# First feed-forward stage begun with six weight blocks per k-tile in six PSUM banks instead of four, with another warm-up operand and another order of the first loads

## Chip, core and metric

The kernel runs on one core of one Trainium2 chip. The metric is device time in microseconds (us); lower is better. Three timed runs of the kernel before gave 985.97, 986.46 and 987.25 us, median 986.46. PE is the matrix engine, DVE the vector engine, ACT the scalar engine, POOL the general engine, SP the engine that only issues transfers here.

## What is computed

A two-layer streaming-encoder trunk on 256 tokens of width 1024, all in float32. The stage that matters here is the first of four feed-forward blocks:

```python
def rms_norm(x, g):
    xf = x.astype(jnp.float32)
    y = xf * lax.rsqrt(jnp.mean(xf * xf, axis=-1, keepdims=True) + NORM_EPS)
    return (y * g.astype(jnp.float32)).astype(x.dtype)

def swiglu(x, w_in, w_out):
    gate, up = jnp.split(x @ w_in, 2, axis=-1)
    return (jax.nn.silu(gate) * up) @ w_out
...
    h = x
    for i in range(DEPTH):
        h = h + 0.5 * swiglu(rms_norm(h, ffn_norm[i, 0]), ffn_w_in[i, 0], ffn_w_out[i, 0])
...
    return rms_norm(h, final_norm)
```

`w_in` is 1024 x 5632 (2816 gate and 2816 up columns), `w_out` 2816 x 1024.

## The kernel before

Activations lie transposed: channels on the 128 partitions in 8 k-tiles (`KD`), the 256 tokens (`T`) along the free axis. Float32 products are made from pairs: a weight block `raw` is rounded to float32r as `whi` on ACT (line 97, or line 1099 for the first blocks), and the remainder `wlo = raw - whi` is taken on DVE (line 101, or line 228). The normalised input has the same two parts in `u` (high part on ACT, line 287; low part on DVE, line 292). For each k-tile and each block of 128 output columns PE runs a pair of matmuls: `whi` times both parts of `u` (512 columns, line 247) and `wlo` times the high part (256 columns, line 248). Here this is called **a pair**; a whole block is 8 pairs.

A feed-forward block has 22 (`KF`) gate blocks and 22 up blocks. Block c makes one PSUM bank `pg` and one bank `pu` (8 pairs each). Seven banks are in rotation, plus one small bank. The 1/rms of a token is not applied to the input but afterwards: DVE multiplies a finished bank by `rb`, the 1/rms of each token laid across all partitions (line 388, result `two`), which frees the bank.

Weights come through the class `Weights`. `plan` lists all weight blocks in order of use. `fetch` issues their transfers on SP (line 88) into four `raw` buffers; `begin` makes `whi` and `pump` makes `wlo` and then calls `fetch`; seven `whi`/`wlo` buffers exist. A block can be begun only if a buffer of the seven is free, that is, if `begun` is below the oldest block still in use (or the next to be got) plus 7.

The first stage is written out by hand (lines 1074 to 1133). `lead` holds, for each k-tile, the input's 256 columns and 4 blocks of weights (gate and up of c = 0 and c = 1): 768 columns, 384 KB, for k = 1 to 7 in one transfer each (line 1078); k = 0 comes in two pieces (lines 188 and 189). Behind them SP issues two weight blocks (line 1080), the two halves of `xt` (line 1082; the same input with tokens on the partitions, called `tokens`), then two more weight blocks. Meanwhile PE runs 16 warm-up matmuls on `warm`, a tile of zeros that DVE writes (lines 1086 to 1090). `first` (line 1106) then works k-tile by k-tile into four banks: for k = 0 the products one kind after the other (line 1110), for each later k four pairs. After k = 1 it squares `tokens` on ACT with a running sum (line 1124, two instructions); after k = 4, `by_token` puts on DVE `v = sums / 1024 + eps` (line 321) and on POOL `rtok = v ** -0.5` (line 326). At k = 1, 3, 5 and 7 `W.pump()` runs. Next come gate and up of c = 2, and then `by_column` (line 331): PE multiplies `rtok`, spread along the free axis, with the identity into the bank `pb`, and ACT copies `pb` to `rb` (line 334). After that the banks of c = 0, 1, 2 are multiplied by `rb` one after the other.

Each engine's instructions stand in one fixed order; the order follows the program text, except that the recording layer may place engines' instructions against each other by readiness.

Of the kernel before, what the change touches and what calls it, by code (L numbers as in the profile page):

```python
# [13 lines left out]
BF16 = mybir.dt.bfloat16  # L14
# [5 lines left out]
P = 128  # L20
D = 1024
T = 256
# [15 lines left out]
G_Q = 72  # L38
G_KV = 74
GAINS = 80  # L40

FV = (H + D) // 3

# [97 lines left out]
def trunk(ctx, tc, xT, xt, pT, pos, freq, bf, lead0, lead1, ffn_in, ffn_out, w_down, w_uq, w_ukv, mla_o,  # L141
# [13 lines left out]

    def plan_ffn(i):

        plan.extend(ffn_in[0, c] for c in range(0 if i else KD // 2))
        plan.extend(ffn_in[i, c] for c in range(0 if i else 4, 2 * KF))
        for d in range(KD):  # L160
            plan.extend(ffn_out[i, d, :, a * P:min(a + KD, KF) * P] for a in range(0, KF, KD))

# [18 lines left out]
    plan.extend(ple_rows[c, k] for c in range(2) for k in range(KD // 2))  # L181


    ROW = T + 4 * P
    lead = big.tile([P, 2 * KD + KD * ROW + 2 * D], F32, name="lead", tag="big")

    a, b = 2 * KD + T + 2 * P, 2 * KD + ROW
# [193 lines left out]
    def ffn(norm, nxt, then=None, first=None, meanwhile=None, later=None, soon=True):  # L381
        hs = big.tile([P, KF, 2, T], F32R, name="hs", tag="big")
        meanwhile = meanwhile or iter(())
        gu, hid = {}, {}

        def evacuate(c, i, ps):
            two = work.tile([P, 2, T], F32, name="two", tag="pair2", bufs=4)
            nc.vector.tensor_mul(two, ps, norm.rb2)  # L388
            gu[c, i] = tmp("gu")
            nc.gpsimd.tensor_add(gu[c, i], two[:, 0, :], two[:, 1, :])  # L390

        def hidden(c):
            h = hid.pop(c)
            split(hs[:, c, 0, :], hs[:, c, 1, :], h)

        def gate(c, ps, pumps=1):
            evacuate(c, 0, ps)
            W.pump(pumps)
            if c:
                hidden(c - 1)  # L400
            sg = tmp("sg")
            nc.scalar.activation(sg, gu.pop((c, 0)), AF.Silu)
            gu[c, 0] = sg

        def up(c, ps, pumps=1):
            evacuate(c, 1, ps)
            hid[c] = tmp("hid")
            nc.gpsimd.tensor_mul(hid[c], gu.pop((c, 0)), gu.pop((c, 1)))  # L408
            W.pump(pumps)
            if c % 2:  # L410
                W.catch_up()
            if first and c == 8:

                nc.sync.dma_start(state, xT)

        waits = [(bank("pg"), bank("pu"))]
        if first:
            waits.append((bank("pg"), bank("pu")))
            first([p for ps in waits for p in ps])
        else:  # L420
            blocks(waits[0], norm.pair)
            W.pump()
            if soon:
                norm.everywhere()
            W.pump()
        at = len(waits)
        for c in range(at, KF):
            pg = bank("pg")
            block(pg, norm.pair)
            if c == at:  # L430
                if soon and not first:
                    norm.turned_back()
                    gate(0, waits[0][0])
                    up(0, waits[0][1])
                    waits.clear()
                else:
                    if not first:
                        norm.everywhere()
                    W.pump()
            else:  # L440
                gate(c, pg)
            pu = bank("pu")
            block(pu, norm.pair)
            if c == at:
                if first:
                    norm.by_column()
                elif not soon:
                    norm.turned_back()
                for x, ps in enumerate(waits):
                    gate(x, ps[0], x)  # L450
                    up(x, ps[1], 0)
                gate(c, pg)
            up(c, pu, 0 if waits and c == at else 1)
        for d in range(KD):
            ps = bank("po")
            for a in range(0, KF, KD):
                w, = W.get()
                part(ps, w, hs, range(a, min(a + KD, KF)), KF - 1, at=lambda k: (k - a) * P)
                W.done(w)
                if a + KD < KF:  # L460
                    W.pump()
                    if d == a == 0:
                        hidden(KF - 1)
                    for _ in range(2):
                        next(meanwhile, None)
            for i in range(2):
                nc.vector.scalar_tensor_tensor(hT[:, d, :], ps[:, i, :], 0.5, hT[:, d, :], op0=ALU.mult, op1=ALU.add)  # L467
            if d < KD - 1:
                nxt.high(d, hT[:, d, :])
                W.pump()  # L470
                nxt.low(d, hT[:, d, :])
                nxt.square(hT[:, d, :])
            else:
                nxt.last(d, hT[:, d, :])
                W.pump()
            W.catch_up()
            if d == 1 and then:
                table(then)
            for _ in range(2):
                next(meanwhile, None)  # L480
            if later:
                later(d)
        for _ in meanwhile:
            pass
# [588 lines left out]

    tokens = lead[:, 2 * KD + KD * ROW:].rearrange("p (t d) -> p t d", t=2)
    steps = lead[:, 2 * KD:2 * KD + KD * ROW].rearrange("p (k n) -> p k n", k=KD)
    W.skip(KD // 2)
    for k in range(1, KD):
        nc.sync.dma_start(steps[:, k, :], lead1[k - 1])
    for t in range(2):
        nc.sync.dma_start(*W.raw())  # L1080
    for t in range(2):
        nc.sync.dma_start(tokens[:, t, :], xt[t])
    W.fetch()
    n0 = Norm(G_FFN, KD, D, table=lead)

    warm = const.tile([P, T], BF16, name="warm")
    nc.vector.memset(warm, 0.0)
    cold = bank("cold", (P, T))
    for _ in range(16):
        nc.tensor.matmul(cold, warm[:, :P], warm, start=True, stop=True)  # L1090
    for k in range(KD):
        if k % 2 == 0:
            hi, lo = W.pair()
        c = slice(k % 2 * 4 * P, (k % 2 + 1) * 4 * P)
        n0.high(k, steps[:, k, :T], vector=k == 0)

        n = 4 * P if k else 2 * P
        for a in range(0, 4 * P, n):
            nc.scalar.activation(hi[:, c][:, a:a + n], steps[:, k, T + a:T + a + n], AF.Copy)  # L1099
        n0.low(k, steps[:, k, :T])  # L1100
        rest(hi[:, c], lo[:, c], steps[:, k, T:])
        if k % 2:
            W.loaded += 1

    def first(ps):
        w, = W.get()

        for x, y, z in ((1, 0, 0), (1, 1, 1), (2, 0, 1)):
            for i, p in enumerate(ps):
                nc.tensor.matmul(p[:, z, :], w[x][:, i * P:(i + 1) * P], n0.pair[:, 0, y, :], start=z == 0,  # L1110
                                 stop=False)
        for k in range(1, KD):
            if k % 2 == 0:
                w, = W.get()
            for i, p in enumerate(ps):
                part(p, w, n0.pair, range(k, k + 1), KD - 1, at=lambda x: (k % 2 * 4 + i) * P)
            if k % 2:
                W.done(w)
                W.pump()
            if k == 1:  # L1120

# [124 lines left out]
def _layout(x, p, positions, ffn_norm, ffn_w_in, ffn_w_out, mix_norm, mla_w_down, mla_q_norm, mla_w_uq,  # L1246
# [15 lines left out]

    w = ffn_w_in.reshape(4, KD, P, 2, KF, P)

    lead = w[0, :, :, :, :2].transpose(0, 1, 3, 2, 4).reshape(KD, P, 4 * P)
    lead = np.concatenate([xT.reshape(P, KD, T).transpose(1, 0, 2), lead], axis=2)
    a["lead0"] = np.ascontiguousarray(np.concatenate([g[:, :2 * KD], lead[0]], axis=1))
    a["lead1"] = np.ascontiguousarray(lead[1:])
# [53 lines left out]
```

## Time and profile before

| | |
|---|---|
| median of three timed runs | 986.46 us |
| profiled execution, own time | 986.36 us |
| span of the profiled execution | 984.5 us |
| time outside the span | 1.86 us |
| 16 warm-up matmuls begin on PE | 1.08 us into the span |
| first weight matmul begins | 4.33 us |
| `pb` begins on PE | 22.96 us |
| granted TensorE clock, mean | 0.999 |

The profile gives, for one execution, the busy time of each engine, a list of who waited for whom, and a timeline. In a timeline row the columns are: start in us from the start of the span, duration in us, engine, line, operation, written tile <- read tiles, shapes, count; in brackets at the end the idle time of the engine before it and what ended that. A name such as `SPq` is the engine's issuing side. KB means 1024 bytes in the sizes of transfers; rates in GB/s are in 10^9 bytes.

### The profile page before, as it was taken

How to read it: one execution, taken by the hardware profiler on the slowest of the kernel's cores; microseconds unless marked ns; L12 is line 12 of the kernel's file. 1: busy time of each engine (PE TensorE's matmuls, PEld its weight loads, DVE VectorE, ACT ScalarE, POOL GpSimd, SP SyncE). 2: the span in 40 equal slices, each digit the busy share in tenths (PEclk: the TensorE clock that was granted, in tenths of full speed). 3: DMA queues.
4: the chain of work that ended last, by engine and by line, in shares of the span. 5: the costliest groups of instructions: out<-in, count | busy, mean ns of one | idle time of the engine just before them, and what ended most of it. 6: DMA issues, size and time to landing. Idle time of an engine off the chain costs nothing.

```text
span 984.5 us, 15920 instructions
## 1 busy us (share of the span) xinstructions
PE 975.1 (99%) x5762; PEld 861.6 (88%) x5762; DVE 741.8 (75%) x1099; ACT 510.2 (52%) x798; POOL 438.1 (44%) x370
## 2 busy tenths in 40 slices
PE   9999999999999999999999999999999999999997
PEld 7888888998988888889888888889889888888886
DVE  6777878686887887666877886666897878876585
ACT  7555544466565454545555454546445555445361
POOL 0777731110377765111477773122231677772120
PEclk9999999999999999999999999999999999999999
DMA  8576666573376665665366666556773666666571
GB/s 317 184 252 209 204 181 188 182 208 117 125 218 213 194 187 177 190 205 172 107 195 211 196 185 196 178 174 224 235 224 112 214 210 204 193 176 198 142 256 54
DMA packets 67006, 187.26 MB, mean 190 GB/s; under 512 B 18628, under 2 KB 21072, under 8 KB 66800
## 3 DMA queue, kind: packets, MB, share of 16 engines
q1 hardware_dynamic: 65904, 183.94, 60.3%
q0 software_dynamic: 448, 1.45, 0.5%
q8 instruction: 46, 0.75, 0.3%
q10 hardware_dynamic: 576, 0.85, 0.3%
q14 instruction: 32, 0.26, 0.1%
HBM read 181.62 MB, written 2.24 MB: 187 GB/s over the span
## 4 chain that ended last, share of the span: by engine, by line
PE 94%; DVE 2%; ACT 1%; issue 1%; DMA 1%; POOL 0%; SPq 0%; POOLq 0%; DVEq 0%; ACTq 0%
PE po L247 17%; PE pu L247 16%; PE pg L247 16%; PE po L248 8%; PE pg L248 8%; PE pu L248 8%; PE ps L247 5%; PE ps L248 2%; PE ps L234 2%; PE ps L232 2%; PE ps L233 2%; PE pv L232 1%; PE pv L234 1%; PE po L557 1%; PE pv L233 1%
## 5 line engine op out<-in xcount | busy, mean ns | idle before, releaser
L101 DVE TENSOR_TENSOR wlo<-raw,whi 128x1024 fp32r<-128x1024 f32 (+2 forms) x339 | 415.0, 1230 | 27.9 <-ACT whi L97 27.1
L97 ACT ACTIVATE whi<-raw 128x1024 fp32r<-128x1024 f32 (+2 forms) x339 | 339.5, 1025 | 91.7 <-PE pg L247 35.5
L390 POOL TENSOR_TENSOR gu<-two 128x256 f32<-128x256 f32 x176 | 233.4, 1327 | 115.4 <-DVE two L388 107.8
L247 PE MATMUL pg<-u,whi 128*128 128x512 f32 x702 | 251.4, 395 | 0.3 <-DVE u L292 0.2
L247 PE MATMUL pu<-u,whi 128*128 128x512 f32 x702 | 250.9, 395 | 0.0
L247 PE MATMUL po<-hs,whi 128*128 128x512 f32 x704 | 246.8, 394 | 0.0
L248 PE MATMUL pg<-u,wlo 128*128 128x256 f32 x702 | 197.1, 281 | 0.6 <-DVE wlo L101 0.5
L248 PE MATMUL po<-hs,wlo 128*128 128x256 f32 x704 | 197.2, 280 | 0.0
L248 PE MATMUL pu<-u,wlo 128*128 128x256 f32 x702 | 196.8, 280 | 0.0
L247 PEld LDWEIGHTS po<-hs,whi 128*128 128x128 f32 x704 | 132.1, 188 | 31.3
L247 PEld LDWEIGHTS pg<-u,whi 128*128 128x128 f32 x702 | 131.8, 188 | 31.7 <-ACT whi L1099 0.5
L247 PEld LDWEIGHTS pu<-u,whi 128*128 128x128 f32 x702 | 131.8, 188 | 31.0
L248 PEld LDWEIGHTS pg<-u,wlo 128*128 128x128 f32 x702 | 132.0, 188 | 1.6 <-DVE wlo L101 0.8
L248 PEld LDWEIGHTS po<-hs,wlo 128*128 128x128 f32 x704 | 132.3, 188 | 0.0
L248 PEld LDWEIGHTS pu<-u,wlo 128*128 128x128 f32 x702 | 132.0, 188 | 0.0
L303 POOL TENSOR_TENSOR acc<-acc,sq 128x256 f32<-128x256 f32 x42 | 45.7, 1089 | 174.5 <-ACT sq L298 153.0
L408 POOL TENSOR_TENSOR hid<-sg,gu 128x256 f32<-128x256 f32 x88 | 112.7, 1281 | 6.9
L228 DVE TENSOR_TENSOR hs<-hid,hs 128x256 fp32r<-128x256 f32 x88 | 59.7, 679 | 57.3 <-ACT hs L224 57.3
L224 ACT ACTIVATE hs<-hid 128x256 fp32r<-128x256 f32 x88 | 36.5, 414 | 115.1 <-POOL hid L408 114.8
L388 DVE TENSOR_TENSOR two<-pg,rb 128x512 f32<-128x512 f32 x88 | 60.3, 685 | 32.1 <-PE pg L248 31.7
L287 ACT ACTIVATE u<-state 128x256 fp32r<-128x256 f32 x47 | 24.0, 511 | 102.9 <-DVE state L467 82.6
L467 DVE SCALAR_TENSOR_TENSOR state<-po,state 128x256 f32<-128x256 f32 x64 | 27.2, 424 | 57.3 <-PE po L248 56.1
(258 smaller groups left out, 1160.1 us busy)
## 6 DMA issues: line engine op xcount, KB each, us to landing
raw<-in_ffn_in_dram SPq DMA_DIRECT2D x172, 512.0 KB, 4.2
raw<-in_ffn_out_dram SPq DMA_DIRECT2D x64, 512.0 KB, 3.7
raw<-in_ffn_out_dram SPq DMA_DIRECT2D x32, 384.0 KB, 3.5
raw<-in_fox_qk_dram SPq DMA_DIRECT2D x16, 512.0 KB, 4.7
raw<-in_mla_o_dram SPq DMA_DIRECT2D x8, 512.0 KB, 4.4
raw<-in_ple_gate_dram SPq DMA_DIRECT2D x8, 512.0 KB, 4.3
raw<-in_fox_o_dram SPq DMA_DIRECT2D x8, 512.0 KB, 4.3
raw<-in_ple_rows_dram SPq DMA_DIRECT2D x8, 512.0 KB, 4.3
```

The costliest lines, as they stand in the source:

```text
L97: self.nc.scalar.activation(self.pairs[i][0][:, c], self.raws[i][:, c], AF.Copy)
L101: self.nc.vector.tensor_sub(lo[:, c], self.raws[i][:, c], hi[:, c].bitcast(F32))
L224: nc.scalar.activation(hi, src, AF.Copy)
L228: nc.vector.tensor_sub(lo, src, hi.bitcast(F32))
L232: nc.tensor.matmul(ps, w[0], x[0], start=first, stop=False)
L233: nc.tensor.matmul(ps, w[1], x[0], start=False, stop=False)
L247: nc.tensor.matmul(ps, hi, x[:, k], start=k == 0, stop=False)
L248: nc.tensor.matmul(ps[:, 1, :], lo, x[:, k, 0, :], start=False, stop=k == last)
L303: nc.gpsimd.tensor_add(new, self.acc, sq)
L388: nc.vector.tensor_mul(two, ps, norm.rb2)
L390: nc.gpsimd.tensor_add(gu[c, i], two[:, 0, :], two[:, 1, :])
L408: nc.gpsimd.tensor_mul(hid[c], gu.pop((c, 0)), gu.pop((c, 1)))
```

## The change

`LEAD = 3` replaces the fixed two: `lead` now holds 6 blocks of weights per k-tile (gate and up of c = 0, 1, 2), 1024 columns or 512 KB for each of k = 1 to 7; the second piece of k = 0, on ACT's queue, grows from 256 to 512 columns. Each k-tile has a `whi`/`wlo` buffer of its own (before, two k-tiles shared one), so the plan skips 8 entries, not 4, and every k-tile counts as one loaded block. `first` works into six banks. `by_column` stands directly behind `first`. The two weight blocks that were issued ahead of `xt` are issued behind it. The warm-up reads the constant 1 that the preamble writes on POOL, and the memset of `warm` goes.

```diff
-        plan.extend(ffn_in[0, c] for c in range(0 if i else KD // 2))
-        plan.extend(ffn_in[i, c] for c in range(0 if i else 4, 2 * KF))
+        plan.extend(ffn_in[0, c] for c in range(0 if i else KD))
+        plan.extend(ffn_in[i, c] for c in range(0 if i else 2 * LEAD, 2 * KF))
...
-    ROW = T + 4 * P
+    ROW = T + 2 * LEAD * P
...
         if first:
-            waits.append((bank("pg"), bank("pu")))
+            waits.extend((bank("pg"), bank("pu")) for _ in range(1, LEAD))
             first([p for ps in waits for p in ps])
+            norm.by_column()
...
             if c == at:
-                if first:
-                    norm.by_column()
-                elif not soon:
+                if not (first or soon):
                     norm.turned_back()
...
-    W.skip(KD // 2)
+    W.skip(KD)
     for k in range(1, KD):
         nc.sync.dma_start(steps[:, k, :], lead1[k - 1])
-    for t in range(2):
-        nc.sync.dma_start(*W.raw())
     for t in range(2):
         nc.sync.dma_start(tokens[:, t, :], xt[t])
     W.fetch()
...
-    warm = const.tile([P, T], BF16, name="warm")
-    nc.vector.memset(warm, 0.0)
+    warm = nc.const_aps.tensor(1.0, [P, T], BF16)
...
-        if k % 2 == 0:
-            hi, lo = W.pair()
-        c = slice(k % 2 * 4 * P, (k % 2 + 1) * 4 * P)
+        hi, lo = (x[:, :2 * LEAD * P] for x in W.pair())
...
-        n = 4 * P if k else 2 * P
-        for a in range(0, 4 * P, n):
-            nc.scalar.activation(hi[:, c][:, a:a + n], steps[:, k, T + a:T + a + n], AF.Copy)
+        for a, b in ((0, 2 * LEAD),) if k else ((0, 2), (2, 2 * LEAD)):
+            nc.scalar.activation(hi[:, a * P:b * P], steps[:, k, T + a * P:T + b * P], AF.Copy)
...
-        rest(hi[:, c], lo[:, c], steps[:, k, T:])
-        if k % 2:
-            W.loaded += 1
+        rest(hi, lo, steps[:, k, T:])
+        W.loaded += 1
...
+        W.done(w)
         for k in range(1, KD):
-            if k % 2 == 0:
-                w, = W.get()
+            w, = W.get()
             for i, p in enumerate(ps):
-                part(p, w, n0.pair, range(k, k + 1), KD - 1, at=lambda x: (k % 2 * 4 + i) * P)
+                part(p, w, n0.pair, range(k, k + 1), KD - 1, at=lambda x: i * P)
+            W.done(w)
             if k % 2:
-                W.done(w)
                 W.pump()
...
-    lead = w[0, :, :, :, :2].transpose(0, 1, 3, 2, 4).reshape(KD, P, 4 * P)
+    lead = w[0, :, :, :, :LEAD].transpose(0, 1, 3, 2, 4).reshape(KD, P, 2 * LEAD * P)
```

The next rows are what SP issues first, from the start of the program, of the kernel before (rows of equal instructions are joined with their count):

```order
L188 DMA lead<-in_lead_dram 128x528
L1078 DMA lead<-in_lead_dram 128x768 x7
L1080 DMA raw<-in_ffn_in_dram 128x1024 x2
L1082 DMA lead<-in_xt_dram 128x1024 x2
L88 DMA raw<-in_ffn_in_dram 128x1024 x21
L414 DMA state<-in_xT_dram 128x2128
```

And the same place of the changed kernel:

```order
L190 DMA lead<-in_lead_dram 128x528
L1079 DMA lead<-in_lead_dram 128x1024 x7
L1081 DMA lead<-in_xt_dram 128x1024 x2
L90 DMA raw<-in_ffn_in_dram 128x1024 x23
L416 DMA state<-in_xT_dram 128x2128
L90 DMA raw<-in_ffn_in_dram 128x1024 x15
```

The two transfers of `xt` moved ahead of all weight blocks, and the seven of `lead` grew by a third.

On ACT, behind the last rounding of `lead`, before (`raw_105` and `raw_107` are the first two weight blocks, `raw_111`, `raw_113` and `raw_214` the next; the row with `sums` is the two squares of `tokens`; `rb` is the copy of `pb`):

```order
L97 ACTIVATE whi_207<-raw_105 128x1024
L97 ACTIVATE whi_210<-raw_107 128x1024
L1124 ACTIVATE lead_80,sums_216<-lead_80 128x1024 x2
L97 ACTIVATE whi_235<-raw_111 128x1024
L97 ACTIVATE whi_261<-raw_113 128x1024
L97 ACTIVATE whi_283<-raw_214 128x1024
L97 ACTIVATE whi_306<-raw_239 128x1024
L334 ACTIVATE rb_332<-pb_329 128x256
```

The same place in the changed kernel, where the weight blocks are, in order, `raw_107`, `raw_109`, `raw_111`, `raw_113` and `raw_229`:

```order
L99 ACTIVATE whi_225<-raw_107 128x1024
L1118 ACTIVATE lead_80,sums_231<-lead_80 128x1024 x2
L99 ACTIVATE whi_258<-raw_109 128x1024
L99 ACTIVATE whi_261<-raw_111 128x1024
L99 ACTIVATE whi_295<-raw_113 128x1024
L99 ACTIVATE whi_325<-raw_229 128x1024
L336 ACTIVATE rb_334<-pb_331 128x256
```

The rounding of the second weight block stood ahead of the squares and now stands behind them; the first one still stands ahead of them.

On DVE, at the place where `v` is made from the sums, before:

```order
L101 TENSOR_TENSOR wlo_208<-raw_105,whi_207 128x1024
L101 TENSOR_TENSOR wlo_211<-raw_107,whi_210 128x1024
L321 TENSOR_SCALAR v_249<-sums_216 128x2
L101 TENSOR_TENSOR wlo_236<-raw_111,whi_235 128x1024
L101 TENSOR_TENSOR wlo_262<-raw_113,whi_261 128x1024
L101 TENSOR_TENSOR wlo_284<-raw_214,whi_283 128x1024
L388 TENSOR_TENSOR two_334<-pg_183,rb_332 128x512
```

And in the changed kernel:

```order
L103 TENSOR_TENSOR wlo_226<-raw_107,whi_225 128x1024
L103 TENSOR_TENSOR wlo_259<-raw_109,whi_258 128x1024
L323 TENSOR_SCALAR v_279<-sums_231 128x2
L103 TENSOR_TENSOR wlo_262<-raw_111,whi_261 128x1024
L103 TENSOR_TENSOR wlo_296<-raw_113,whi_295 128x1024
L103 TENSOR_TENSOR wlo_326<-raw_229,whi_325 128x1024
L390 TENSOR_TENSOR two_376<-pg_189,rb_334 128x512
```

The order of kinds is the same: `v` stands behind the remainders of two weight blocks in both. What changed is on ACT: the second of those remainders now reads a rounding that stands behind the squares.

More of the change, by code (lines that the diff above doesn't have):

```diff
@@ L40 @@
 GAINS = 80
+LEAD = 3
 FV = (H + D) // 3
```

## Prediction

> **What bounds the kernel now.** I read the page's head and its chain of waits first, then PE's list of waits, then the timeline of the first 27 us engine by engine.
>
> ```profile
> span 984.5 us, 15920 instructions
> PE 975.1 (99%) x5762; PEld 861.6 (88%) x5762; DVE 741.8 (75%) x1099; ACT 510.2 (52%) x798; POOL 438.1 (44%) x370
> PE 94%; DVE 2%; ACT 1%; issue 1%; DMA 1%; POOL 0%; SPq 0%; POOLq 0%; DVEq 0%; ACTq 0%
> ```
>
> PE is busy 99% of the span and 94% of the chain that ended last, so a change pays only where it moves PE, and what PE loses early is not made up later. PE's own waits over the whole span are few:
>
> ```profile
> PE cold L1090 <- DVE warm L1087: 1.1, 1, 1.1
> PE pg L248 <- DVE wlo L101: 0.5, 1, 0.5
> PE pg L247 <- DVE u L292: 0.2, 1, 0.2
> PE pg L248 <- DVE wlo L228: 0.2, 1, 0.2
> PE po L557 <- ACT ptS L545: 0.2, 1, 0.2
> ```
>
> Here the columns are total us, number of waits, longest. The change touches the first, third and fourth, all of them in the first 10 us. So the gain has a ceiling near 2 us, and the question is what new wait can stand against it. A tile's 1/rms is the candidate: `pb` on PE waits for `rtok` on POOL, and everything on PE stands behind `pb`. These rows are POOL, DVE and PE at that place:
>
> ```profile
> 18.52 0.71 POOL L326 TENSOR_TENSOR rtok<-v,mhalf 128x2 f32<-128x2 f32 x1 [16.88 <-DVE v L321]
> 18.19 0.17 DVE L321 TENSOR_SCALAR v<-sums 128x2 f32<-128x2 f32 x1 [1.34 <-ACT lead L1124]
> 22.96 0.61 PE L331 MATMUL pb<-ident,rtok 128*128 128x128 f32 x4
> 23.32 0.48 PE L247 MATMUL pg<-u,whi 128*128 128x512 f32 x1
> 26.21 0.40 PE L247 MATMUL pu<-u,whi 128*128 128x512 f32 x1
> ```
>
> `rtok` was ready at 18.52 + 0.71 = 19.23, and PE asked for it at 22.96: the chain has 3.73 us to spare before.
>
> **How late PE asks after the change.** Ahead of `pb` stands the same amount of work: before, 4 blocks x 8 k-tiles + 16 pairs of c = 2 = 48 pairs; after, 6 x 8 = 48. (For k = 0, three matmuls of 256 columns stand for a pair.) What differs is when the early tiles arrive.
>
> ```profile
> 4.97 0.51 ACT L287 ACTIVATE u<-lead 128x256 fp32r<-128x256 f32 x1 [0.53 <-DMA lead<-in_lead_dram]
> 5.39 0.61 ACT L1099 ACTIVATE whi<-lead 128x512 fp32r<-128x512 f32 x1
> 7.27 0.51 ACT L287 ACTIVATE u<-lead 128x256 fp32r<-128x256 f32 x1 [1.27 <-DMA lead<-in_lead_dram]
> ...
> 8.34 0.69 DVE L228 TENSOR_TENSOR wlo<-lead,whi 128x512 fp32r<-128x512 f32 x1
> ...
> 9.08 0.39 PE L248 MATMUL pg<-u,wlo 128*128 128x256 f32 x1 [0.17 <-DVE wlo L228]
> ...
> 9.30 0.39 PE L247 MATMUL pu<-u,whi 128*128 128x512 f32 x1
> ```
>
> From 9.30 PE runs 39 pairs (3 left of k = 2, 20, 16) until 22.96: 0.350 us a pair. The waits for transfers are at 4.97 (k = 1, behind 264 + 128 + 384 = 776 KB) and 7.27 (k = 2, behind 1,160 KB). After, k = 1 ends behind 264 + 256 + 512 = 1,032 KB; between those two points that is about 4.97 + 2.30 x 256/384 = 6.5. Then 0.42 to the rounding, 0.83 for 768 columns (0.61 for 512, 1.06 for 1024 in the row below), 0.97 for `wlo` of 768 (0.69 for 512, 1.25 for 1024): `wlo` at 8.8, the second pair at 9.0, and 41 pairs more: PE asks for `pb` at 9.0 + 14.35 = **23.4**. The bounds are k = 1 at 5.6 and at 7.27: 22.5 to 24.1. So the six banks alone are worth between 0.5 gained and 1.2 lost, best value 0.4 lost: the wait at k = 2 goes, one at k = 1 of the same kind comes.
>
> **When `rtok` is ready after the change.** This decides. The rows of ACT and DVE on the path, before:
>
> ```profile
> 13.26 1.06 ACT L97 ACTIVATE whi<-raw 128x1024 fp32r<-128x1024 f32 x1 [0.22 <-DMA raw<-in_ffn_in_dram]
> 14.53 1.06 ACT L97 ACTIVATE whi<-raw 128x1024 fp32r<-128x1024 f32 x1 [0.21 <-DMA raw<-in_ffn_in_dram]
> 15.76 1.06 ACT L1124 ACTIVATE lead<-lead 128x1024 f32<-128x1024 f32 x1 [0.17 <-DMA lead<-in_xt_dram]
> 16.73 0.19 ACT L1124 ACTIVATION_READ_ACCUMULATOR lead<-lead 128x1 f32 x1
> 17.01 1.06 ACT L1124 ACTIVATE lead<-lead 128x1024 f32<-128x1024 f32 x1
> 17.98 0.18 ACT L1124 ACTIVATION_READ_ACCUMULATOR lead<-lead 128x1 f32 x1
> 19.83 1.06 ACT L97 ACTIVATE whi<-raw 128x1024 fp32r<-128x1024 f32 x1 [1.67 <-DMA raw<-in_ffn_in_dram]
> 21.18 1.06 ACT L97 ACTIVATE whi<-raw 128x1024 fp32r<-128x1024 f32 x1 [0.29 <-DMA raw<-in_ffn_in_dram]
> ...
> 14.35 2.50 DVE L101 TENSOR_TENSOR wlo<-raw,whi 128x1024 fp32r<-128x1024 f32 x2 [0.33 <-ACT whi L97]
> ```
>
> The transfers are one behind the other, and ACT waits for each. `xt` is fetched sooner in order but not in bytes: before, 392 + 7 x 384 + 2 x 512 + 2 x 512 = 5,128 KB end with it; after, 520 + 7 x 512 + 2 x 512 = 5,128 KB. It lands when it did, by 17.0. But on ACT the first weight block's rounding stands ahead of the squares in both, and that block now lands *behind* `xt`, as the 5,640th KB: before, that place was the third block's, and ACT got it at 19.83. So I take 19.83 for it. From there, by the rows:
>
> - rounding of block one at 19.83; the next ACT instruction 0.97 later (16.73 - 15.76, the same size): first square 20.80
> - two squares 15.76 to 18.16, so 2.40: done 23.20
> - rounding of block two starts there (its data, as the fourth block's before, came by 21.18)
> - its remainder on DVE 1.09 later (13.26 to 14.35): 24.29, taking 1.25: 25.54
> - `v` behind it in DVE's order, although its sums are ready since 23.20: 25.54
> - POOL starts 0.33 after `v` starts (18.19 to 18.52) and takes 0.71: **`rtok` at 26.58**, against 19.23 before.
>
> PE, asking at 23.4, stands for 3.2 us. `pb` at 26.62 instead of 22.96: **+3.66 us**.
>
> **What is late behind it.** The fourth up block (`pu` of c = 3) reuses the bank of the first gate block, so it waits for the first `two`, as before:
>
> ```profile
> 20.92 3.82 DVE L101 TENSOR_TENSOR wlo<-raw,whi 128x1024 fp32r<-128x1024 f32 x3 [2.56 <-ACT whi L97]
> 25.05 0.69 DVE L388 TENSOR_TENSOR two<-pg,rb 128x512 f32<-128x512 f32 x1 [0.31 <-ACT rb L334]
> 24.65 0.37 ACT L334 ACTIVATE rb<-pb 128x256 f32<-128x256 f32 x1
> ```
>
> Before, `two` ended at 25.74 and PE needed the bank at 26.21. After, `v` ends at 25.71, three remainders (3.82) stand ahead of `two` until 29.53, `two` ends 30.22; PE gets there at 26.62 + (26.21 - 22.96) = 29.87. So **+0.35** more. ACT's copy `rb` is not later than DVE: three roundings of 0.97 from 24.17 end at 27.1, `rb` is done by 27.5. Behind that the banks are freed faster than PE fills them, as before. Weight blocks only gain time while PE stands.
>
> **The remaining edits.** The memset of `warm` held PE until 1.08; DVE's first instruction of the program is at 0.80, so warm-up can begin up to 0.28 earlier. With the early matmuls at half pace for as long, that is worth at most 0.15 us, and the 128 KB more on ACT's queue can cost the first matmul about 0.3 (131,072 bytes at about 400 GB/s). Both lie ahead of the wait at `pb`, which swallows either sign, so I put them at 0; without that cover they are -0.15 and +0.3. Later order on DVE and ACT differs where two-block counts became one-block counts; PE's only later waits are 0.5 and 0.2, so I allow 0.5 either way and take 0.
>
> **Sum.** Against the profiled execution's own 986.36 (span 984.5 + 1.86; the median of the timed runs is 986.46, the same for this purpose): 3.66 + 0.35 = +4.0, so **990.3 us**, +0.40%.
>
> **Rivals.** *The late block lands earlier.* The third block's landing at 19.83 is 2.8 us behind `xt`, where its neighbours took 1.25. In that stretch one transfer of the instruction queue q8 appears, and the mean rate stays high:
>
> ```profile
> DMA packets 337, 1.25 MB, mean 416 GB/s; under 512 B 35, under 2 KB 35, under 8 KB 336
> ...
> q8 instruction: 1, 0.02, 2.1%
> ```
>
> 512 KB at 416 GB/s is 1.26 us. If that hindrance falls on another transfer, block one lands at 17.0 + 1.25 = 18.25 and everything moves with it: `rtok` 25.0, +2.1 at `pb`, +0.3 behind: 988.8. For it: the instructions' transfer follows PE's progress, which is a little different now. Against it: by my count PE is at nearly the same instruction then.
>
> *No stall, so not slower.* `rtok` comes before PE asks if block one lands before 23.4 - 6.8 = 16.6. Then only the early terms count: +0.4 (-0.5 to +1.2), 986.8. Larger packets could carry the lead faster than the early dip before, but 5,640 KB at 416 GB/s (13.9 us) behind a first landing wait of 3.7 us leaves little room. That the change works as its parts suggest, with the early waits gone and the clock up 0.3 us sooner, lies at the lower end of this case: 985.9 or less.
>
> *The clock drops in the stall.* Before, the matmuls after warm-up keep a slow pace until 5.5, that is 4.5 us after PE began:
>
> ```profile
> 5.33 0.41 PE L1110 MATMUL pg<-u,whi 128*128 128x256 f32 x1
> 5.54 0.37 PE L1110 MATMUL pu<-u,whi 128*128 128x256 f32 x1
> 5.75 0.28 PE L1110 MATMUL pg<-u,whi 128*128 128x256 f32 x1
> 5.87 0.28 PE L1110 MATMUL pu<-u,whi 128*128 128x256 f32 x1
> ```
>
> The starts are 0.21 apart, then 0.12. If PE's 3.2 us of standing put it back into the slow pace for again 4.5 us, half of that, 2.2 us, is lost: 992.5. No row here shows PE idle for so long, so this trace cannot say. [...]
>
> **How the numbers follow.** Forecast 990.3: 0.60. Earlier landing, 988.8: 0.20. No stall, 986.8: 0.10. Clock drop, 992.5: 0.10. The range leaves out the third and most of the fourth: 987.9 to 991.6. A measurement of this kernel tells about 0.2%, 2.0 us, from no change. Slower by more than that: all of the first, most of the second, the fourth: 0.84; within it: 0.13; faster: 0.03.
>
> **What would show it.** In the profile after: the first rounding of a `raw` block ahead of the squares with idle time before it ended by a transfer, near 19.8; the second remainder on DVE directly ahead of `v`, near 24.3; `pb` on PE with idle time of about 3 us ended by POOL's `rtok`, as the largest of PE's waits; `pu` of c = 3 waiting 0.3 for `two`. Wrong would be `rtok` ready before PE asks for it, or PE asking later than 24.1.

## The result and the profile after

The changed kernel takes **990.77 us** (median of 6 runs, 989.64 to 993.59) against 986.30 (6 runs, 985.67 to 987.25) for the kernel before on the same chip: ratio 1.0049, 95% interval 1.0039 to 1.0060. It is 4.5 us slower, and the predicted 990.3 lies 0.5 us off. But only a part of the loss lies where the prediction put it, as the traces and the experiments show. The profile of after below is of the execution that took 993.59 us, the longest of the six.

The first lines are the head of the page of after and the group of DVE's remainders of raw weight blocks (L103 here, L101 before): busy time, mean ns, and, behind the second bar, the idle time ahead of them and what ended most of it. The last line is the same group of before.

```profile
span 991.8 us, 15934 instructions
PE 977.5 (99%) x5764; PEld 863.4 (87%) x5764; DVE 752.1 (76%) x1096; ACT 510.1 (51%) x796; POOL 441.5 (45%) x370
...
PE 88%; DVE 5%; DMA 3%; ACT 2%; issue 2%; POOL 1%; SPq 0%; POOLq 0%; ACTq 0%; DVEq 0%
...
L103 DVE TENSOR_TENSOR wlo<-raw,whi 128x1024 fp32r<-128x1024 f32 (+2 forms) x337 | 416.7, 1243 | 56.1 <-ACT whi L99 55.0
```

```profile
L101 DVE TENSOR_TENSOR wlo<-raw,whi 128x1024 fp32r<-128x1024 f32 (+2 forms) x339 | 415.0, 1230 | 27.9 <-ACT whi L97 27.1
```

PE is still busy 99% of the span, but its busy time has grown by 2.4 us, so some of its matmuls ran slower. And the remainders wait twice as long for ACT's roundings, 55.0 us against 27.1. By their rows 26 of these 28 us lie in the first 220 us, far beyond the stage that was changed; behind 300 us the two kernels wait alike (24.8 and 23.1). PE's own waits after (us in total, number, longest):

```profile
PE pb L333 <- POOL rtok L328: 2.2, 1, 2.2
PE pt L544 <- DVE pr L522: 2.2, 1, 2.2
PE cold L1088 <- PEq L1302: 0.8, 1, 0.8
PE pg L1104 <- ACT whi L1094: 0.5, 1, 0.5
PE pg L250 <- DVE wlo L103: 0.5, 1, 0.5
PE pkv L234 <- DVE u L287: 0.5, 1, 0.5
```

The first is the forecast one; the second and the last lie at 200 to 226 us, in the first attention stage (called MLA), where nothing was forecast. (`pkv` is the bank of its key and value projection, `psc` holds the attention scores, `pr` the probabilities made from them, `pt` their transpose.) These are the rows of ACT, DVE, POOL and PE around the first:

```profile
17.71 1.06 ACT L99 ACTIVATE whi<-raw 128x1024 fp32r<-128x1024 f32 x1 [2.61 <-DMA raw<-in_ffn_in_dram]
18.67 1.04 ACT L1118 ACTIVATE lead<-lead 128x1024 f32<-128x1024 f32 x1
...
20.75 3.92 ACT L99 ACTIVATE whi<-raw 128x1024 fp32r<-128x1024 f32 x4
```

```profile
21.83 1.23 DVE L103 TENSOR_TENSOR wlo<-raw,whi 128x1024 fp32r<-128x1024 f32 x1 [1.80 <-ACT whi L99]
22.97 0.16 DVE L323 TENSOR_SCALAR v<-sums 128x2 f32<-128x2 f32 x1
23.04 3.49 DVE L103 TENSOR_TENSOR wlo<-raw,whi 128x1024 fp32r<-128x1024 f32 x3
```

```profile
23.29 1.54 POOL L328 TENSOR_TENSOR rtok<-v,mhalf 128x2 f32<-128x2 f32 x1 [21.65 <-DVE v L323]
```

```profile
24.88 0.71 PE L333 MATMUL pb<-ident,rtok 128*128 128x128 f32 x4 [2.21 <-POOL rtok L328]
...
25.86 0.63 PE L249 MATMUL pg<-u,whi 128*128 128x512 f32 x1
26.29 0.41 PE L250 MATMUL pg<-u,wlo 128*128 128x256 f32 x1
26.50 0.63 PE L249 MATMUL pg<-u,whi 128*128 128x512 f32 x1
```

The squares stand behind the first raw rounding, `v` behind the second remainder, and PE for 2.21 us at `pb`. Then a pair takes 26.50 - 25.86 = 0.64 us instead of 0.35. The windows of one us (start and end, length, busy time and count of PE, its weight loads, DVE, ACT and POOL, granted clock, share and rate of DMA) say why:

```profile
24.00:25.00 1.00, 0.12 (x1) 0.12 (x2) 1.00 (x2) 0.67 (x1) 0.83 (x1) 1.00 0.84 246
25.00:26.00 1.00, 1.00 (x7) 0.96 (x8) 1.00 (x2) 0.37 (x1) 0.00 (x0) 0.83 0.95 352
26.00:27.00 1.00, 1.00 (x5) 0.81 (x4) 1.00 (x2) 0.41 (x2) 0.00 (x0) 0.50 0.88 336
...
29.00:30.00 1.00, 1.00 (x8) 0.88 (x6) 0.72 (x1) 0.34 (x1) 1.00 (x1) 0.96 0.93 381
```

The granted clock is 0.50 from 25.67 to 29.08, 3.41 us; by the table below that costs 1.6 us. The same happens a second time from 227.05 to 230.47, behind PE's wait at `pt`. There DVE is the place to look. The first piece is DVE after, the second DVE before at the same point of the program:

```profile
195.12 1.22 DVE L103 TENSOR_TENSOR wlo<-raw,whi 128x1024 fp32r<-128x1024 f32 x1 [1.53 <-ACT whi L99]
...
197.15 2.08 DVE L103 TENSOR_TENSOR wlo<-raw,whi 128x768 fp32r<-128x768 f32 x2
199.16 0.87 DVE L468 SCALAR_TENSOR_TENSOR state<-po,state 128x256 f32<-128x256 f32 x2
200.06 0.35 DVE L287 TENSOR_SCALAR u<-state 128x256 fp32r<-128x256 f32 x1
...
205.10 1.22 DVE L103 TENSOR_TENSOR wlo<-raw,whi 128x1024 fp32r<-128x1024 f32 x1 [2.48 <-ACT whi L99]
206.24 0.15 DVE L325 SCALAR_TENSOR_TENSOR v<-pst,eps 128x2 f32<-128x2 f32 x1
...
215.80 1.29 DVE L737 TENSOR_TENSOR kqv<-ps,rbs 128x512 f32<-128x512 f32 x2 [3.02 <-DMA rbs<-row]
...
220.92 2.36 DVE L103 TENSOR_TENSOR wlo<-raw,whi 128x1024 fp32r<-128x1024 f32 x2
223.19 0.29 DVE L502 CUSTOM_DVE_ANT_0 pr<-psc,chunks 128x128 f32<-128x128 f32 x1
```

```profile
191.85 0.88 DVE L467 SCALAR_TENSOR_TENSOR state<-po,state 128x256 f32<-128x256 f32 x2 [2.38 <-PE po L248]
192.77 0.35 DVE L285 TENSOR_SCALAR u<-state 128x256 fp32r<-128x256 f32 x1
...
193.56 1.49 DVE L101 TENSOR_TENSOR wlo<-raw,whi 128x768 fp32r<-128x768 f32 x1
...
198.18 1.24 DVE L101 TENSOR_TENSOR wlo<-raw,whi 128x1024 fp32r<-128x1024 f32 x1
199.41 0.16 DVE L323 SCALAR_TENSOR_TENSOR v<-pst,eps 128x2 f32<-128x2 f32 x1
...
207.82 1.29 DVE L736 TENSOR_TENSOR kqv<-ps,rbs 128x512 f32<-128x512 f32 x2
...
212.84 2.45 DVE L101 TENSOR_TENSOR wlo<-raw,whi 128x1024 fp32r<-128x1024 f32 x2
215.78 0.29 DVE L501 CUSTOM_DVE_ANT_0 pr<-psc,chunks 128x128 f32<-128x128 f32 x1 [0.48 <-PE psc L784]
```

Before, DVE sat idle until PE's last `po` came, and the remainder followed the critical `u`. After, a remainder waits 1.53 us for its rounding, two more stand behind it and ahead of the state's sum, and `u` comes late; that is the wait at `pkv`.

The wait at `pt` begins with `v`, a value per token from which 1/rms is made. Before, the remainder ahead of `v` read a rounding that ACT had begun at 193.15. After, it stands idle 2.48 us until a rounding that ACT begins only at 204.02, and `v` comes 6.8 us later than before, where PE was some 4 us late. The 1/rms then goes through two transfers (`row`, `rbs`) and is laid across the partitions. Before, `rbs` is there when DVE comes; after, DVE stands 3.02 us for it, and from there on it has no idle time until the scores' maximum, on which `pr` and PE's `pt` hang. (The two remainders ahead of that maximum stand there in both kernels and are not the difference.) The experiments below bear this out: `again`, `order` and `bphase` wait 3.56, 3.17 and 2.39 us for `rbs`, `phase` not at all and `both` 0.18.

To see how much each place costs, PE's matmuls were matched between the traces, counted back from the last one. The table gives by how many us the matmul with the same number of matmuls behind it starts later than in the profile of before, at five of its times; the kernels other than after are the experiments below. Each column is one execution.

| at (us of before) | after | `again` | `order` | `phase` | `both` | `best2` | `bphase` | `small` |
|---|---|---|---|---|---|---|---|---|
| 17 | -0.45 | -0.42 | -0.44 | -0.57 | -0.50 | -0.48 | -0.71 | +0.63 |
| 33 | +3.58 | +1.40 | +0.11 | +1.25 | +0.66 | -0.46 | -0.71 | +1.27 |
| 190 | +3.23 | +1.06 | -0.23 | +0.91 | +0.32 | -0.80 | -0.60 | +1.27 |
| 240 | +8.02 | +4.72 | +4.77 | +0.97 | +0.38 | -0.73 | +5.29 | +1.28 |
| 975 | +7.21 | +3.53 | +4.13 | +0.16 | -0.78 | -1.63 | +5.29 | +1.33 |

After stands 3.6 us late at 33 us (1.92 at `pb`, which began at 24.88 and not at 22.96, and 1.64 in the half clock), loses another 4.8 between 190 and 240, and gets about 1 us back slowly.

**Why the MLA stage.** The code has a reason that the rows fit. The loop `gate(x, ps[0], x)` asks the weight pipeline for x blocks at each waiting column x: 0 + 1 = 1 with the two columns of before, 0 + 1 + 2 = 3 with the three of after. Counted in the order of the program, before has 5 blocks ready and 6 begun each time PE takes one, from c = 3 on. After has 7 and 7, from c = 4 on: all seven buffers are full, ACT can round a new block only when PE gives one up, and DVE's remainder waits for ACT each time. In the trace this lasts until about 220 us, where the additional idle time ends.

### The profile page after: what moved, and what is told of

Read it like the earlier page. It is cut to its first block, busy times and chain, and to the rows that moved or that the text cites. A ratio compares the mean times of both kernels' runs of the same rounds, so it can differ in the third digit from the quotient of the medians.

```text
span 991.8 us, 15934 instructions
## 1 busy us (share of the span) xinstructions
PE 977.5 (99%) x5764; PEld 863.4 (87%) x5764; DVE 752.1 (76%) x1096; ACT 510.1 (51%) x796; POOL 441.5 (45%) x370
## 4 chain that ended last, share of the span: by engine, by line
PE 88%; DVE 5%; DMA 3%; ACT 2%; issue 2%; POOL 1%; SPq 0%; POOLq 0%; ACTq 0%; DVEq 0%
PE pg L249 16%; PE pu L249 16%; PE po L249 15%; PE pg L250 8%; PE pu L250 8%; PE po L250 8%; PE ps L249 5%; PE ps L250 2%; DVE wlo L103 2%; PE ps L234 1%; PE ps L235 1%; PE ps L236 1%; ACT whi L99 1%; DMA raw<-in_ffn_in_dram 1%; PE pv L234 1%
## 5 line engine op out<-in xcount | busy, mean ns | idle before, releaser
L103 DVE TENSOR_TENSOR wlo<-raw,whi 128x1024 fp32r<-128x1024 f32 (+2 forms) x337 | 416.7, 1243 | 56.1 <-ACT whi L99 55.0
L99 ACT ACTIVATE whi<-raw 128x1024 fp32r<-128x1024 f32 (+2 forms) x337 | 337.1, 1024 | 100.2 <-PE pg L249 39.6
L392 POOL TENSOR_TENSOR gu<-two 128x256 f32<-128x256 f32 x176 | 230.0, 1307 | 113.4 <-DVE two L390 105.8
L305 POOL TENSOR_TENSOR acc<-acc,sq 128x256 f32<-128x256 f32 x42 | 48.4, 1152 | 171.9 <-ACT sq L300 150.5
L230 DVE TENSOR_TENSOR hs<-hid,hs 128x256 fp32r<-128x256 f32 x88 | 65.5, 744 | 40.0 <-ACT hs L226 40.0
L404 ACT ACTIVATE sg<-gu 128x256 f32<-128x256 f32 x88 | 36.8, 418 | 74.9 <-POOL gu L392 74.9
```

Of the source, the lines that this page charges most:

```text
L99: self.nc.scalar.activation(self.pairs[i][0][:, c], self.raws[i][:, c], AF.Copy)
L103: self.nc.vector.tensor_sub(lo[:, c], self.raws[i][:, c], hi[:, c].bitcast(F32))
L230: nc.vector.tensor_sub(lo, src, hi.bitcast(F32))
L305: nc.gpsimd.tensor_add(new, self.acc, sq)
```

## The experiments

The theories: (1) the wait at `pb` comes from the order behind the late raw blocks; (2) the MLA losses come from the two extra blocks in the pipeline; (3) the half clock follows PE's idling. Against (2): the six banks, or the changed transfers, make them.

**The change once more.**

> The changed kernel as it is, profiled and timed once more. In its first profile PE stood 2.2 us at `pb` and then ran at a granted clock of 0.50 for 3.4 us (25.7 to 29.1), and again stood 2.2 us at `pt` (L544, 226 us) and again had 3.4 us at 0.50. Theory: the two waits are built into the order of the instructions and come back (PE `pb` 2.0 to 2.5 us behind `rtok`; PE `pt` 1 to 3 us behind `pr`), the half clock is a matter of when an execution meets them and comes back in some executions only: 989.5 to 992 us, ratio to the kernel before 1.003 to 1.006. Rival: the half clock belongs to these waits and appears in both places every time.

992.20 us (4 runs, 989.91 to 993.55), ratio 1.0055 (1.0042 to 1.0069), just above the expected 992. In the profiled run (989.91) the waits come back, 1.5 us at `pb` (under the expected 2.0 to 2.5) and 2.2 at `pt`, and the clock doesn't drop until PE's work ends: the table has +1.8 from 17 to 33, and +3.7 from 190 to 240. So both waits come without a half clock too, which speaks against the rival. The changed kernel's times spread over 3.6 us here, those of before over 1.3.

**The order in the first stage alone.**

```
             W.done(w)
-            if k % 2:
-                W.pump()
             if k == 1:
...
-            if k == 4:
                 n0.by_token()
+            if k % 2:
+                W.pump()
```

> The changed kernel with ACT's two squares and DVE's `v` put ahead of the first raw weight block in program order (both at k = 1 of the first stage, ahead of the pump). If the order behind the late raw blocks makes the wait at `pb`, `rtok` is ready near 18 to 19.5 us, `pb` starts when PE asks for it, 22.2 to 23.2, its wait and the half clock behind it are gone, and the later losses in the MLA stage stay: 987.0 to 989.0 us, 1.7 to 3.6 below the changed kernel. If POOL itself (its `rtok` took 1.54 us where it had taken 0.71) or the late xt makes the wait, `pb` still waits over 1 us for `rtok` and the time stays at 990 to 991.

990.64 us (5 runs, 990.49 to 990.80), ratio 1.0042 (1.0029 to 1.0055). The mechanism at `pb` was right and the expected time was not. `rtok` is ready at 17.16 + 0.71 = 17.87 and PE doesn't wait at `pb`; but the kernel is as slow as the changed one. The time went into MLA: +5.0 us there in the profiled run, which shows the half clock behind `pt`. All five runs lie within 0.3 us at a mean clock of 0.996 to 0.997, so the other four probably had it as well:

```profile
PE pt L544 <- DVE pr L522: 2.2, 1, 2.2
```

```profile
223.00:224.00 1.00, 1.00 (x7) 0.88 (x6) 0.45 (x3) 0.48 (x2) 0.00 (x0) 0.75 1.00 365
224.00:225.00 1.00, 1.00 (x6) 0.91 (x4) 0.24 (x2) 1.00 (x5) 0.00 (x0) 0.50 0.99 370
```

So the wait that carried the forecast is not needed for the loss.

**Two weight blocks fewer ahead.**

```
-                    gate(x, ps[0], x)
+                    gate(x, ps[0], int(x == 1))
```

> The changed kernel with the three waiting columns' gates pumping 0, 1, 0 blocks instead of 0, 1, 2, so that the weight pipeline stands, as before, 5 blocks ready and 6 begun ahead of PE, not 7 and 7. If the two extra blocks make the losses at 195 to 230 us (DVE's remainder waits for ACT's rounding, which waits for PE to free a buffer, and `v`, `u` and `pr` stand behind the remainder), the wait of PE's `pt` for `pr` (2.2 us) and that of `pkv` for `u` (0.5) go back to at most 0.3 each, the idle time of DVE L103 behind ACT's `whi` falls from 55 to about 28 us, the wait at `pb` stays at 2 us, and the time is 987 to 989.3, 1.5 to 4 below the changed kernel. If six banks or the different transfers make those losses, `pt` still waits over 1.5 us and the time stays at 990 to 991.

**986.52 us** (11 runs, 986.26 to 987.33), ratio 1.0002 (0.9993 to 1.0011): this one number takes away all but 0.3 us of the loss. PE's largest wait is the one at `pb`, and the remainders' idle time is back:

```profile
PE pb L333 <- POOL rtok L328: 1.5, 1, 1.5
```

```profile
L103 DVE TENSOR_TENSOR wlo<-raw,whi 128x1024 fp32r<-128x1024 f32 (+2 forms) x337 | 413.1, 1232 | 30.9 <-ACT whi L99 30.1
```

In the table the step between 190 and 240 is 0.06 us. The time fell under the expected 987: the wait at `pb` was 1.5 us and not 2, and no half clock followed it in the profile.

**Both edits.**

> The two edits of `order` and `phase` together in the changed kernel. If these two places are the whole loss, it lies at the kernel before or a little under it: 985.0 to 987.0 us, ratio to the kernel before 0.9985 to 1.0005, with no wait of PE over 1.2 us. If the six banks themselves, the constant in the warm-up or the order of the transfers cost something of their own, more than 1 us of the 4.3 remains: above 987.3.

985.91 us (11 runs, 985.23 to 986.55), ratio 0.9996 (0.9987 to 1.0004), as expected; six banks cost nothing that is left. The order is worth 0.6 us here and not the 1.5 of the wait (and the intervals of `phase` and `both` overlap). A wait took the place of the one removed: a remainder that starts at 24.88 stands ahead of the first `two`.

```profile
PE pu L249 <- DVE two L390: 0.9, 1, 0.9
```

**Two blocks more in the kernel before.**

```
-                    gate(x, ps[0], x)
+                    gate(x, ps[0], 3 * x)
```

> The kernel before with one number changed: its second waiting column pumps 3 blocks instead of 1, so that the weight pipeline stands 7 ready and 7 begun ahead of PE, as in the changed kernel; banks, transfers and warm-up stay those of before. If the two extra blocks alone make the losses at 195 to 225 us, PE's `pt` (L543) waits 1.5 to 2.5 us for `pr`, the idle time of DVE's remainders behind ACT's `whi` doubles to about 55 us, and the time is 989.5 to 991.5 (3.7 us, and 1.7 more where the half clock follows), ratio 1.0033 to 1.0053. If it takes the six banks or the changed transfers as well, it stays at 986 to 987.

**992.16 us** (5 runs, 991.36 to 993.59) against 986.57, ratio 1.0059 (1.0047 to 1.0072), even a little above the range. With four banks, the old transfers and the old warm-up, the MLA loss is there in full, and a half clock from 200.01 to 203.42 behind the first wait:

```profile
PE pkv L232 <- DVE u L285: 2.0, 1, 2.0
PE pt L543 <- DVE pr L521: 1.6, 1, 1.6
```

```profile
L101 DVE TENSOR_TENSOR wlo<-raw,whi 128x1024 fp32r<-128x1024 f32 (+2 forms) x339 | 418.9, 1242 | 53.3 <-ACT whi L97 52.6
```

This and `phase` settle theory (2) from both sides: the two blocks alone make the loss, and without them it is gone.

**The two small edits in the kernel before.** xt's two transfers ahead of the two weight blocks, and the warm-up from the constant without a memset.

> The kernel before with the two small edits of the change alone: xt's transfers issued ahead of the first two weight blocks, and the warm-up from the constant 1 without its memset. If neither costs or gains anything by itself, 985.9 to 986.5 us, and `rtok` is ready by 20.5, ahead of PE's asking at 22.96, although the first rounding of a raw block comes before the squares with its data behind xt here too (its data end with the 4,616th and 5,128th KB, not with the 5,640th and 6,152nd). If the order of the transfers alone makes the wait at `pb`, that wait is over 1 us and the time is 987.5 to 989.

987.02 us (11 runs, 986.22 to 987.81) against 986.57, ratio 1.0005 (0.9996 to 1.0014): 0.45 us above, which this measurement cannot tell from nothing. (In the profiled execution, of 987.64 us, PE is 1.3 us later than before from 20 us on, behind a wait of 0.9 for `u` and one of 0.4 for the first weight block's remainder.) PE doesn't wait at `pb`, as expected, but `rtok` is ready only at 21.19 + 0.71 = 21.90, not by 20.5: of the 3.73 us that the chain had to spare before, the two small edits take 2.7. In after the six blocks per k-tile push the raw blocks back by another 1,024 KB, and `rtok` comes another 2.9 us later; 0.8 of these are POOL's longer instruction. No run has the six blocks without the two edits.

**Filling PE's wait at `pt`.** `order` with

```
             pt = bank("pt", (P, 3 * P))
+            for _ in range(0 if filled else 18):
+                nc.tensor.matmul(pt[:, :T], warm[:, :P], warm, start=True, stop=True)
+            filled.append(h)
```

(`filled` is an empty list at the start, so that only the first head's `pt` gets them.)

> The kernel `order` with 18 bf16 matmuls of 256 columns of the constant 1 into the bank of `pt`, ahead of its first transpose and overwritten by it, so that PE is busy for some 1.9 of the 2.2 us in which it waits there. In `order` PE idled 220.4 to 222.6 and had the granted clock 0.50 from 223.49 to 226.91. If the idle time makes the half clock, `pt` comes when it came, the half clock is gone, and the time falls by 1.3 to 1.8 us from 990.64, to 988.8 to 989.4. If the half clock comes from something else (load of the DMA engines, of DVE), it stays: 990.4 to 991, or more if the matmuls delay `pt`.

991.86 us (5 runs, 990.09 to 992.74): no gain, and by that number the theory would fall. The trace shows that the run did not test it cleanly. Behind `pt` the clock stayed at 1.00; but the wait of `pkv` for `u` was 1.4 us in this execution, against 0.6 in `order`, and the half clock followed that, 198.92 to 202.34. A further wait of 1.2 us, of `pst` for POOL's `acc`, stands at 956 us in it. So the next run fills both places.

**Filling both waits.** Ten such matmuls more, into the bank of `pr`, ahead of the last k-tile of `pkv`.

> `ptfill` once more with 10 further bf16 matmuls of 256 columns (1.1 us) of the constant 1 into the bank of `pr`, before the pair in which PE waited 1.4 us for `u` at 198 us there (0.6 in `order`), since the half clock of `ptfill` (198.92 to 202.34) followed that wait and not the one at `pt`, which was filled. If a window of 3.41 us with 1.5 us of idle PE or more is what halves the clock, no half clock is left between 10 and 975 us, and no execution can lose 1.7 us in it: median 988.6 to 990.0, below both `order` (990.64) and `ptfill` (991.86), and a spread under 1.6 us. If filling PE does not matter, half-clock windows remain and the median stays at 990.5 to 992.

989.14 us (6 runs, 988.44 to 993.07) against 986.55, ratio 1.0036 (1.0023 to 1.0048): 1.5 below `order` and 2.7 below `ptfill`, and no half clock in the middle of its profile. But the interval overlaps that of `order` (1.0029 to 1.0055) and of `ptfill` (1.0040 to 1.0065), so a gain in time is not shown. Nor was the spread as expected: one run at 993.07 lies far outside, and the other five spread over 2.0 us; what happened in the one isn't known.

The fourteen profiles together say more. In these traces the clock's changes lie on a grid of 3.413 us whose place differs from execution to execution (in after 5.19, 25.67, 29.08, 227.05 and 230.47 us, which are 6, 1, 58 and 1 such steps apart; in before 5.73 and 981.95, 286 steps apart). For each grid window the idle time of PE's rows was added up; these are the longest between 10 and 950 us:

| kernel | window, us | PE idle in it, us | clock in the next |
|---|---|---|---|
| after | 22.25 to 25.67 | 2.21 | 0.50 |
| `order` | 220.08 to 223.49 | 2.18 | 0.50 |
| after | 223.64 to 227.05 | 2.16 | 0.50 |
| `bphase` | 196.60 to 200.01 | 1.66 | 0.50 |
| `phase` | 21.16 to 24.57 | 1.53 | 1.00 |
| `again` | 21.15 to 24.56 | 1.53 | 1.00 |
| `ptfill` | 195.51 to 198.93 | 1.47 | 0.50 |
| `again` | 222.53 to 225.95 | 1.39 | 1.00 |
| `rotraw` (below) | 707.81 to 711.22 | 1.23 | 1.00 |
| `bphase` | 220.49 to 223.91 | 1.08 | 1.00 |

In these profiles the clock halved behind each window with 1.66 us or more and behind none with 1.39 or less, and between lie both. `again` stood as long at `pt` as after did, but an edge of the grid cut its wait into 0.78 and 1.39, and its clock stayed.

**One weight block moved in `both`.** The pump ahead of the up block of c = 3 goes behind the first gate column.

```
                     if not first:
                         norm.everywhere()
-                    W.pump()
+                        W.pump()
...
-                    gate(x, ps[0], int(x == 1))
+                    gate(x, ps[0], int(x < 2) if first else x)
```

> The kernel `both` with one weight block more moved: the pump ahead of the up block of c = 3 goes behind the first gate column, so that DVE's first `two` no longer stands behind that block's remainder (0.9 us of PE's wait for `two` in `both`), and the pipeline still stands 5 ready and 6 begun. If that wait was late work on DVE only, it falls under 0.2 us and the time is 984.8 to 985.4, ratio to the kernel before 0.9985 to 0.9992. If what is pumped later makes a later wait of the same size, it stays at 985.7 to 986.2.

985.11 us (11 runs, 984.65 to 987.25), ratio 0.9989 (0.9981 to 0.9998); no wait for `two` is left. Seven times lie at 984.65 to 985.26 and four at 985.85 to 987.25, and the profiled run (986.87) is one of the four. Its matmuls at 9 us still have the half pace; the second row is `both` at the same time:

```profile
8.85 0.63 PE L249 MATMUL pg<-u,whi 128*128 128x512 f32 x1
```

```profile
8.83 0.39 PE L249 MATMUL pu<-u,whi 128*128 128x512 f32 x1
```

**Eighteen warm-up matmuls instead of sixteen in `best`.**

> The kernel `best` with 18 warm-up matmuls in place of 16, to fill the 0.4 to 0.6 us that PE waits for its first rounding at 4.3 us. In the profile of `best` (986.87 us, seven of its eleven executions lay at 984.65 to 985.26) the full clock came only at 10.01 us, where the other profiles had it at 3.93 to 5.92. If that late grant, made by the gap ahead of the first matmul, is what separates its two groups of times, no execution lies above 986 and the median is 984.6 to 985.2. If the gap does not matter, there are still executions at 986 to 987.3.

**984.71 us** (11 runs, 984.49 to 985.31) against 986.55, ratio 0.9983 (0.9974 to 0.9992). No run lies above 985.4, and the first weight matmul follows the warm-up without a gap. That agrees with the expectation; the late full clock itself was seen in one profile only, so that it made the other three longer times of `best` is not shown:

```profile
0.77 4.00 PE L1088 MATMUL cold<-const-bfloat16-1.0 128*128 128x256 bf16 x18 [0.77 <-PEq L1301]
4.79 0.55 PE L1104 MATMUL pg<-u,whi 128*128 128x256 f32 x1
```

This version is 1.8 us faster than the kernel before on the same chip, and some 6 us faster than the change as made, by medians of different chips.

**The slow gain.** In the table after, `again`, `order`, `phase`, `both` and `best2` gain 1.0 to 1.5 us on before outside the waits, spread over the feed-forward stages; `bphase` and `small` don't. Two kernels without any added instruction tried the place of the weights in SBUF:

```
     W = Weights(nc, wp, plan)
+    for _ in range(2):
+        for x in ("whi", "wlo"):
+            W.pool.tile([P, KD * P], F32R, name=x, bufs=W.PAIRS)
```

> The kernel before with two whi/wlo buffers taken and never used ahead of the first, so that every later weight block lies in the buffer (of the 7 in rotation) in which the changed kernel has it; no instruction is added or moved. In all six profiles with six banks PE gains 1.1 to 1.4 us on the kernel before between 33 and 900 us, evenly over the feed-forward stages, and in the two other profiles with four banks nothing. If the place of the weights in SBUF makes that, this kernel's PE shows the same gain from 33 to 900 us, and the time is 985.0 to 985.6. If it is something else, the gain is under 0.2 us and the time 986.2 to 986.8.

> As `rot`, and with two raw buffers taken as well, so that the 4 raw buffers too stand as in the changed kernel. If it takes the places of raw and whi/wlo together, PE gains 1.1 to 1.4 us from 33 to 900 us here and not in `rot`: 985.0 to 985.6. If the places are not the cause, no gain here either: 986.2 to 986.8.

Neither showed the gain, and both times lie above both expected ranges. `rot` took 987.64 us (11 runs) against 986.55, ratio 1.0012 (1.0003 to 1.0021); against before its PE stood at -0.55 at 33 us, -0.70 at 240 and +0.84 at 900. `rotraw` took 987.81, ratio 1.0014 (1.0005 to 1.0023), with the same slope and one wait of 2.0 us for a transfer. So taking other buffers did change PE's pace, by 1.5 us over 660, but in the other direction; what gives the six-bank kernels their gain stays open.

## Why the prediction was right and wrong

**The bound.** Right: PE sets the end, and what it loses early isn't made up.

**When PE asks for `pb`.** Forecast 23.4, measured 24.88 - 2.21 = 22.67, inside the bounds. The six banks gain 0.3 here instead of losing 0.4: the k-tile k = 1 came at 5.66 and not at 6.5, near the lower bound of 5.6. The packets of `lead` are larger, 4 KB for 3, and took 162 ns each against 143 (means of the 429 and 527 begun in the first 8 us): 25.3 bytes per ns against 21.5.

**When `rtok` is ready.** The mechanism was right: block one's rounding ahead of the squares, the second remainder directly ahead of `v`. The size was off. The landing was taken as 19.83, from the third block before, and was 17.71; this is the rival "the late block lands earlier", even beyond its 18.25. The transfer of instructions that this rival speaks of came at 17.19 us, behind 88 of PE's matmuls; before it came at 17.73, behind 87. The prediction had the better number and didn't use it: 5,640 KB at 416 GB/s (13.9 us) behind 3.7 us make 17.6. POOL took 1.54 us, not 0.71. `rtok` came at 24.83 instead of 26.58, and `pb` was 1.92 us late instead of 3.66 (1.11 in `phase`, where it began at 24.07).

**The wait of `pu` for `two`, +0.35.** Not there in after, where `two` ended at 27.13 and PE came at 29.77 at its half clock, nor in `again` at the full clock; 0.9 in `both`, where `rtok` is early. The queue behind `v` was seen rightly.

**The clock.** The rival at 0.10 happened in the profiled execution. Its price was put at 2.2 us, from 4.5 us of slow pace, and was 1.6, from 3.41. That the forecast itself holds nothing for the clock behind a stall of 3.2 us was the author's estimate; no row of before shows such a stall. Measured: behind 2.21 us of idle PE in a window of 3.413 the granted clock fell to 0.50 in after, and behind 1.47 in `ptfill`.

**The remaining edits.** The bound of +0.3 for the longer first transfer was too small: the first weight matmul started at 4.84 instead of 4.33. The wait swallowed it, as said.

**Later order, taken as 0 with 0.5 either way.** This step failed, and it holds the larger part of the result. It named the place ("where two-block counts became one-block counts") and sized it by PE's later waits of 0.5 and 0.2 us. But those were small *because* the pipeline had two free buffers. The runs put 3.7 us (`again`) to 5.9 us (`bphase`, its half clock included) in its place, and `phase`, which undoes it, lies 0.3 us from the kernel before. A number that says how far one engine runs ahead is a state that outlives its stage, here from the first stage into MLA at some 220 us, and it was read as a local change of order.

So the sum of 4.0 was right by chance: forecast 4.0 at `pb` and 0 in MLA, measured 1.3 to 1.4 at 33 us (`phase`, `again`) and 3.7 in MLA where the clock holds, less some 1.5 of slow gain until 900 us, plus 1.6 for each half clock.

## What to carry to other kernels

When an edit changes how many blocks a pipeline is pumped, count what is ready and what is begun at every take in both versions before pricing any wait: a pipeline filled to its last buffer makes each refill wait for the consumer (here the remainders stood 55.0 us for ACT's roundings against 27.1). The price appeared here 170 us later, where small urgent work shared the refilling engine. When a wait is to be judged, look at what stands directly ahead of the tiny instruction that ends it, and at the granted clock behind it. In the two profiles with cheap matmuls in PE's longer waits the granted clock stayed at 1.00 behind them (`ptfill` behind `pt`, 223 to 227 us) and was 0.999 over the span (`fill2`); that this saves time is not shown here.

## What was not expected of the hardware

The clock's windows, above: 3.413 us on a grid of their own. In after the wait of 2.21 us at `pb` lay in one window, and 1.64 us more were lost behind it; in `again` a wait of 2.17 at `pt` lay in two, 0.78 and 1.39, and the clock stayed. The rows from 1.47 to 1.53 went either way. The start of the full clock behind the warm-up lies on the same grid in before and after (5.73 and 5.19 us, above). It came at 3.51 to 6.48 us in thirteen profiles and at 10.01 in `best`, where PE idled 0.43 us in the window from 3.19 to 6.60; but `order` and after got it behind a window with 0.49, so idle time alone doesn't explain that grant.

POOL's `rtok`, 128 x 2 values, took 0.71 us in the eleven profiles in which DVE ran nothing beside it (in `small` a remainder began in its last 0.08 us), and 1.54 in the three in which a remainder followed `v` at once (after, `again`, `phase`). In after the first of the three remainders ran from 23.04 to about 24.27, POOL's instruction from 23.29 to 24.83. The author's reading is that the remainder held POOL up; that is not shown, as no run here took the remainder alone away at that place.

Two unused `whi`/`wlo` buffers ahead of the others made the whole kernel 1.1 us longer (`rot`, ratio 1.0003 to 1.0021), with every instruction the same; why is open.
